# Six tiles of the second output block ahead of the gated mixer, and kept tiles for the down projection's last rows

## The chip, the cores and the metric

The kernel runs on one core of one Trainium2 chip. The time is device microseconds of one execution, taken as the median of several; the profile is one more execution, recorded by the hardware profiler. The engines of a core work side by side and wait for each other by semaphores: TensorE (PE, matrix products; its weight loads are PEld), VectorE (DVE), ScalarE (ACT), GpSimd (POOL), and SyncE (SP), which here only issues transfers between the device's memory (DRAM) and the on-chip memory. Products are added up in a separate small memory, PSUM.

## The reference

One decoder layer on 256 tokens of width 2048, in float32. A norm, one wide input projection, and two mixers (a gated delta rule over 16 heads and a causal pooling mixer) that are gated and added; an output projection with a residual; a norm, a gated MLP of width 5632 with a causal convolution, a down projection with a residual; a last norm.

```python
def reference(x, norm_mix_w, w_in, ..., w_out, norm_ffn_w, w_up, conv_ffn_w, conv_ffn_b, w_down, norm_final_w):
    ...
        mixed = jax.nn.sigmoid(g_a) * y_a + jax.nn.sigmoid(g_b) * y_b
        x = x + jnp.einsum('bsd,de->bse', mixed, w_out[l])
        h = rmsnorm(x, norm_ffn_w[l])
        gate, up = jnp.split(jnp.einsum('bsd,df->bsf', h, w_up[l]), 2, axis=-1)
        gate = causal_dwconv(gate, conv_ffn_w[l]) + conv_ffn_b[l]
        x = x + jnp.einsum('bsf,fd->bsd', jax.nn.gelu(gate, approximate=False) * up, w_down[l])
    return rmsnorm(x, norm_final_w)
```

## The kernel before

All weights pass once through one stream of tiles. A tile is 256 rows by 512 columns of a weight (two blocks of 128 rows, 512 KB). The list `srcs` fixes the order of the stream. For each tile, SP issues a load into one of four `raw` buffers (L112); ACT casts it into one of three `whi` buffers (L121); DVE subtracts that from `raw` into one of three `wlo` buffers (L128). `hi` and `lo` together carry the float32 value through products that keep fewer bits. `weights()` hands out the next tile and prepares the stream two tiles further.

A product of float32 quality is three matmuls: high part times `hi`, low part times `hi`, high part times `lo`. `gemm_a` (L158 to L160) does this for a block of 512 output columns: for each tile two row blocks and two halves of 128 tokens, twelve matmuls. A block of columns needs eight tiles where the depth is 2048, and its sums lie in one of two PSUM tiles `psm`.

Instructions are written in program order, and a scheduler with a simulated timeline orders them within each engine when the kernel is built. Each engine then works its own list off in order.

The mixers run in four groups of four heads. Each group yields four of the sixteen row blocks that the output projection multiplies (`mhi`, `mlo`). For the last group, `gated()` (L840, L841: the products that end in `sz`) and `mixed()` (eight PE transposes of `sz`, L203; the cast L853; the subtraction L854) come late. So the output projection starts early with what is ready: six tiles of column block 0 and two of block 1 (L864), whose rows belong to groups 0 to 2. The last two tiles of a block, rows of the fourth group, can be used only after `mixed()`. Then `xt`, the input x for the residual, is loaded by four transfers on ACT's queue (L872), and each finished block is added to it (L882, DVE), squared for the norm (L885, ACT), transposed (L891, PE), cast (L895) and split (L896).

The MLP follows, and then the down projection. It has 22 row steps `kp` of four tiles each, one for each block c of 512 columns; the sums of four blocks and two token halves t fill all eight PSUM banks. `down_part` (L945 to L947) is six matmuls: one tile, one token half. For the last row step, the tile of block 0 is used as it comes; the other three are used first for all of half 0 and then for half 1. Behind each half: the sum with the residual (L962, DVE) and the square (L964, ACT) per block, the mean over four columns (L966, L967, DVE), the power −1/2 (L968, POOL), the products with the last norm's weights `nfin` and with the scale (L971 and L975, DVE; L978, ACT), and four stores issued by SP (L979).

Of the kernel before, what the change touches and what calls it, by code (L numbers as in the profile page):

```python
# [7 lines left out]
F32 = mybir.dt.float32  # L8
# [5 lines left out]
P = 128  # L14
# [19 lines left out]
def kernel(  # L34
# [32 lines left out]
    def nm(s):  # L67
        cnt[0] += 1
        return f"{s}_{cnt[0]}"
# [45 lines left out]
    def begin(n):  # L115
        while len(made) < min(len(srcs), n):
            load(len(made) + 1)
            raw = loads[len(made)]
            shape = list(raw.shape)
            hi = wpool.tile(shape, F32R, tag="whi", name=nm("whi"))  # L120
            nc.scalar.copy(hi, raw)  # L121
            if shape[1] == 8:
                lo = None
                nc.vector.tensor_tensor(hi[:, :, 32:64], raw[:, :, 0:32], hi[:, :, 0:32].bitcast(F32),
                                        op=ALU.subtract)
            else:
                lo = wpool.tile(shape, F32R, tag="wlo", name=nm("wlo"))
                nc.vector.tensor_tensor(lo, raw, hi.bitcast(F32), op=ALU.subtract)  # L128
            made.append((hi, lo))

# [744 lines left out]
    ssq4 = cpool.tile([P, 2, 4], F32, tag="ssq4", name="ssq4b")  # L875
    for c in range(4):
        if c < 2:
            ps = gemm_a(at(mhi), at(mlo), KD, range((6, 2)[c], 8), early[c])
        else:
            ps = gemm_a(at(mhi), at(mlo), KD)  # L880
        xs = xt[:, :, c * 512 : (c + 1) * 512]
        nc.vector.tensor_tensor(xs, xs, ps, op=ALU.add)  # L882
        for t in range(2):
            jk = cpool.tile([P, 512], F32, tag="sqj", name=nm("sqj"))
            nc.scalar.activation(jk, xs[:, t, :], AF.Square, accum_out=ssq4[:, t, c : c + 1])  # L885
        for k2 in range(2):
# [59 lines left out]
            mm(acc[c][t], ll(k, t), hi[:, kk, :], start=False, stop=False)  # L946
            mm(acc[c][t], lh(k, t), lo[:, kk, :], start=False, stop=(k == KF - 1))  # L947

    LAST = KF // 2 - 1
# [6 lines left out]
    ssq5 = cpool.tile([P, 2, 4], F32, name="ssq5")  # L956
    for t in range(2):
        for c in range(1, 4):
            down_part(LAST, c, t, *ws[c - 1])
        for c in range(4):  # L960
            xs = xt[:, t, c * 512 : (c + 1) * 512]
            nc.vector.scalar_tensor_tensor(xs, acc[c][t], rs2[:, t : t + 1], xs, op0=ALU.mult, op1=ALU.add)  # L962
            jk = cpool.tile([P, 512], F32, tag="sqj", name=nm("sqj"))
            nc.scalar.activation(jk, xs, AF.Square, accum_out=ssq5[:, t, c : c + 1])  # L964
        rs = cpool.tile([P, 1], F32, name=nm("rs"))
        nc.vector.tensor_reduce(rs, ssq5[:, t, :], axis=mybir.AxisListType.X, op=ALU.add)  # L966
        nc.vector.tensor_scalar(rs, rs, 1.0 / D, EPS, op0=ALU.mult, op1=ALU.add)  # L967
        nc.gpsimd.tensor_tensor(rs, rs, epsx[:, 0:1], op=ALU.pow)  # L968
        for c in (2, 3):
            xs = xt[:, t, c * 512 : (c + 1) * 512]  # L970
            nc.vector.tensor_tensor(xs, xs, nfin[:, c * 512 : (c + 1) * 512], op=ALU.mult)  # L971
        for c in (0, 2, 1, 3):
            xs = xt[:, t, c * 512 : (c + 1) * 512]
            if c < 2:
                nc.vector.scalar_tensor_tensor(xs, xs, rs, nfin[:, c * 512 : (c + 1) * 512],  # L975
                                               op0=ALU.mult, op1=ALU.mult)
            else:
                nc.scalar.activation(xs, xs, AF.Copy, scale=rs)  # L978
            nc.sync.dma_start(out[0, t * P : (t + 1) * P, c * 512 : (c + 1) * 512], xs)  # L979


# [29 lines left out]
```

## Time and profile before

| | us |
|---|---|
| median of 3 runs | 1581.47 (1581.29 to 1581.65) |
| the profiled execution | 1581.2 |
| its span, first to last instruction | 1579.4 |
| PE busy | 1565.1 |
| DVE busy | 1066.2 |
| ACT busy | 745.4 |
| output projection: first and last matmul | 733.6 to 835.5 |
| last load of the weight stream issued | 1551.8 |

The span is shorter than the execution by what lies ahead of the first and behind the last recorded instruction. Matmuls overlap in PE's pipeline, so a matmul of 0.39 us can start every 0.23 us; the pitch of the starts tells PE's pace, and the busy time tells only whether it stood still. The granted clock was 0.998 over the span. In a row of a timeline, the bracket at the end names how long the engine had been idle before and what released it.

### The profile page before, as it was taken

The numbers are of one execution on the slowest core, as the hardware profiler recorded it, in microseconds if no ns is written. First come the engines' busy times: TensorE is split into PE (matmuls) and PEld (weight loads), VectorE is DVE, ScalarE is ACT, GpSimd is POOL, SyncE is SP. The second block draws the span as 40 slices with busy tenths as digits, with TensorE's granted clock in tenths as the row PEclk, the third lists the DMA queues.
The fourth block names the chain that finished last, engine by engine and source line by source line (L and its number), as shares of the span: only waits on it lengthen the run. The fifth ranks groups of instructions, "written<-read, shape, count | busy, mean of one in ns | idle before, by whom it ended". The sixth has DMA issues, their size and how long they took to land.

```text
span 1579.4 us, 21330 instructions
## 1 busy us (share of the span) xinstructions
PE 1565.1 (99%) x8086; PEld 1315.5 (83%) x8086; DVE 1066.2 (68%) x1619; ACT 745.4 (47%) x954; POOL 45.0 (3%) x69
## 2 busy tenths in 40 slices
PE   9999999999999999999999999999999999999997
PEld 8878888888878888788788888888888888888885
DVE  6897758885798657785556667766666667444445
ACT  6454445544555445544454544444444444434344
POOL 3010000000000000000000000000000000000000
PEclk9999999999999999999999999999999999999999
DMA  8776657675667647775656666666666666666663
GB/s 261 207 233 187 185 160 209 206 213 170 180 210 205 199 137 208 218 199 169 197 181 183 188 188 188 191 191 189 186 188 188 188 190 214 195 196 191 196 189 132
DMA packets 167925, 304.22 MB, mean 193 GB/s; under 512 B 19187, under 2 KB 22275, under 8 KB 167695
## 3 DMA queue, kind: packets, MB, share of 16 engines
q1 hardware_dynamic: 165088, 298.36, 64.1%
q10 hardware_dynamic: 2734, 4.51, 0.9%
q8 instruction: 63, 1.03, 0.3%
q14 instruction: 40, 0.32, 0.1%
HBM read 297.56 MB, written 5.27 MB: 192 GB/s over the span
## 4 chain that ended last, share of the span: by engine, by line
PE 96%; DVE 1%; DMA 1%; issue 1%; ACT 0%; DVEq 0%; POOLq 0%; POOL 0%; SPq 0%
PE psm L160 14%; PE psm L159 14%; PE psm L158 14%; PE psm L182 10%; PE psg L182 10%; PE psg L183 5%; PE psm L183 5%; PE psg L945 3%; PE psg L946 3%; PE psg L947 3%; PE psm L945 2%; PE psm L947 2%; PE psm L946 2%; PE psm L285 1%; PE psg L620 1%
## 5 line engine op out<-in xcount | busy, mean ns | idle before, releaser
L128 DVE TENSOR_TENSOR wlo<-raw,whi 128x1024 fp32r<-128x1024 f32 x528 | 645.1, 1223 | 421.0 <-ACT whi L121 412.1
L121 ACT CAST whi<-raw 128x1024 fp32r<-128x1024 f32 x530 | 557.6, 1053 | 737.9 <-PE psm L159 308.4
L160 PE MATMUL psm<-wlo,xhl 128*128 128x512 f32 x864 | 339.5, 393 | 0.7 <-DVE wlo L128 0.7
L158 PE MATMUL psm<-whi,xhl 128*128 128x512 f32 x864 | 339.0, 392 | 0.0
L159 PE MATMUL psm<-whi,xhl 128*128 128x512 f32 x864 | 338.4, 392 | 0.0
L182 PE MATMUL psm<-fhl,whi 128*128 128x512 f32 x704 | 246.2, 396 | 0.0
L182 PE MATMUL psg<-fhl,whi 128*128 128x512 f32 x704 | 238.0, 394 | 0.0
L183 PE MATMUL psm<-fhl,wlo 128*128 128x256 f32 x704 | 194.4, 279 | 0.0
L160 PEld LDWEIGHTS psm<-wlo,xhl 128*128 128x128 f32 x864 | 162.3, 188 | 34.3 <-DVE wlo L128 1.4
L159 PEld LDWEIGHTS psm<-whi,xhl 128*128 128x128 f32 x864 | 162.2, 188 | 33.4
L158 PEld LDWEIGHTS psm<-whi,xhl 128*128 128x128 f32 x864 | 162.3, 188 | 32.9 <-issue 0.2
L183 PE MATMUL psg<-fhl,wlo 128*128 128x256 f32 x704 | 178.7, 279 | 0.0
L182 PEld LDWEIGHTS psm<-fhl,whi 128*128 128x128 f32 x704 | 131.4, 188 | 30.5
L182 PEld LDWEIGHTS psg<-fhl,whi 128*128 128x128 f32 x704 | 129.2, 188 | 24.2
L183 PEld LDWEIGHTS psg<-fhl,wlo 128*128 128x128 f32 x704 | 132.5, 188 | 6.9
L183 PEld LDWEIGHTS psm<-fhl,wlo 128*128 128x128 f32 x704 | 132.5, 188 | 1.1
L945 PE MATMUL psg<-whi,hhi 128*128 128x512 f32 x176 | 68.6, 390 | 0.0
L945 PE MATMUL psm<-whi,hhi 128*128 128x512 f32 x176 | 68.5, 389 | 0.0
L946 PE MATMUL psm<-whi,hlo 128*128 128x512 f32 x176 | 68.5, 389 | 0.0
L946 PE MATMUL psg<-whi,hlo 128*128 128x512 f32 x176 | 68.5, 389 | 0.0
L947 PE MATMUL psm<-wlo,hhi 128*128 128x512 f32 x176 | 68.5, 389 | 0.0
L947 PE MATMUL psg<-wlo,hhi 128*128 128x512 f32 x176 | 61.7, 389 | 0.0
(241 smaller groups left out, 1489.7 us busy)
## 6 DMA issues: line engine op xcount, KB each, us to landing
raw<-in_w_in_dram SPq DMA_DIRECT2D x226, 512.0 KB, 4.3
raw<-in_w_up_dram SPq DMA_DIRECT2D x176, 512.0 KB, 4.5
raw<-in_w_down_dram SPq DMA_DIRECT2D x88, 512.0 KB, 4.4
raw<-in_w_out_dram SPq DMA_DIRECT2D x32, 512.0 KB, 3.9
mv<-vrow SPq DMA_DIRECT2D x12, 512.0 KB, 5.1
taps<-in_conv_qkv_w_dram SPq DMA_DIRECT2D x16, 256.0 KB, 6.0
raw<-in_pool_w_dram SPq DMA_DIRECT2D x8, 512.0 KB, 6.0
x<-in_x_dram SPq DMA_DIRECT2D x4, 512.0 KB, 8.2
```

The costliest lines, as they stand in the source:

```text
L121: nc.scalar.copy(hi, raw)
L128: nc.vector.tensor_tensor(lo, raw, hi.bitcast(F32), op=ALU.subtract)
L158: mm(ps[:, t, :], lh(k, t), hi[:, kk, :], start=(k == 0), stop=False)
L159: mm(ps[:, t, :], ll(k, t), hi[:, kk, :], start=False, stop=False)
L160: mm(ps[:, t, :], lh(k, t), lo[:, kk, :], start=False, stop=(k == nk - 1))
L182: mm(ps[f], hi[:, kk, fs], rhl(k), start=(k == 0), stop=False, skip_group_check=True)
L183: mm(ps[f][:, 1, :], lo[:, kk, fs], rhl(k)[:, 0, :], start=False, stop=(k == nk - 1), skip_group_check=True)
L285: mm(ps_k0[:, t, :], part(k, t), w[:, kk, :], start=(k == 0 and w is hi and part is xh), stop=(k == KD - 1 and w is lo))
L620: mm(pg0, kq[:, h, 0, 0:P], kq[:, h, :, :], start=True, stop=True)
L945: mm(acc[c][t], lh(k, t), hi[:, kk, :], start=(k == 0), stop=False)
L946: mm(acc[c][t], ll(k, t), hi[:, kk, :], start=False, stop=False)
L947: mm(acc[c][t], lh(k, t), lo[:, kk, :], start=False, stop=(k == KF - 1))
```

## The change

Three edits.

In the output projection, six tiles of block 1 come ahead of `gated()` and `mixed()` in program order instead of two, and the list of the stream is changed to match: six tiles of block 0, six of block 1, the last two of block 0, the last two of block 1.

In the down projection, the four tiles of the last row step (`LAST`, 21) are taken from the end of the stream and put in behind the row steps 9, 12, 15 and 18, one each. Their `hi` and `lo` go to buffers of their own, `khi` and `klo`, in the places that held row blocks of the MLP's result which the down projection has by then used (`mtile` 0 to 7).

At the end, the last two row steps are done block by block for each token half: for block c the tile of row step 20 and then the kept tile of row step 21. The tile of block 0 in row step 20 is used for both halves at once. Sum, square and product with `nfin` follow each block as it is done; for block 3 the product with `nfin` is merged with the scale. The mean is made from a partial sum over three blocks (`part`) and the fourth square. Blocks 2 and 3 are scaled on DVE, blocks 0 and 1 on ACT; three stores go to SP's queue and the fourth to ACT's.

```diff
-    srcs += outw[0][:6] + outw[1][:2] + outw[0][6:] + outw[1][2:] + outw[2] + outw[3]
+    srcs += outw[0][:6] + outw[1][:6] + outw[0][6:] + outw[1][6:] + outw[2] + outw[3]
...
-    srcs += [down[c][kp] for kp in range(KF // 2) for c in range(4)]
+    LAST = KF // 2 - 1
+    KEEP = (9, 12, 15, 18)
+    kept = {}
+    for kp in range(LAST):
+        srcs += [down[c][kp] for c in range(4)]
+        if kp in KEEP:
+            kept[len(srcs)] = KEEP.index(kp)
+            srcs.append(down[KEEP.index(kp)][LAST])
...
-            hi = wpool.tile(shape, F32R, tag="whi", name=nm("whi"))
+            keep = kept.get(len(made))
+            hi = wpool.tile(shape, F32R, tag="whi", name=nm("whi")) if keep is None else \
+                mtile(keep, shape, F32R, nm("khi"))
...
-    early = [gemm_a(at(mhi), at(mlo), KD, range(n)) for n in (6, 2)]
+    early = [gemm_a(at(mhi), at(mlo), KD, range(n)) for n in (6, 6)]
...
-            ps = gemm_a(at(mhi), at(mlo), KD, range((6, 2)[c], 8), early[c])
+            ps = gemm_a(at(mhi), at(mlo), KD, range(6, 8), early[c])
...
-    for kp in range(LAST + 1):
-        for c in range(4 if kp < LAST else 1):
+    wk = []
+    for kp in range(LAST - 1):
+        for c in range(4):
             w = weights()
             for t in range(2):
                 down_part(kp, c, t, *w)
-    ws = [weights() for c in range(3)]
+        if kp in KEEP:
+            wk.append(weights())
+    ws = []
+    for c in range(4):
+        ws.append(weights())
+        if c == 0:
+            for t in range(2):
+                down_part(LAST - 1, c, t, *ws[c])
...
     for t in range(2):
-        for c in range(1, 4):
-            down_part(LAST, c, t, *ws[c - 1])
         for c in range(4):
+            if c:
+                down_part(LAST - 1, c, t, *ws[c])
+            down_part(LAST, c, t, *wk[c])
...
+            if c < 3:
+                nc.vector.tensor_tensor(xs, xs, nfin[:, c * 512 : (c + 1) * 512], op=ALU.mult)
+            if c == 2:
+                nc.vector.tensor_reduce(part[:, ts], ssq5[:, t, 0:3], axis=mybir.AxisListType.X, op=ALU.add)
+                nc.vector.tensor_scalar(part[:, ts], part[:, ts], 1.0 / D, EPS, op0=ALU.mult, op1=ALU.add)
+        nc.vector.tensor_scalar(rs[:, ts], ssq5[:, t, 3:4], 1.0 / D, part[:, ts], op0=ALU.mult, op1=ALU.add)
+        nc.gpsimd.tensor_tensor(rs[:, ts], rs[:, ts], epsx[:, 0:1], op=ALU.pow)
+        scaled(2, nc.vector, nc.sync)
+        scaled(0, nc.scalar, nc.sync)
+        scaled(3, nc.vector, nc.sync)
+        scaled(1, nc.scalar, nc.scalar)
```

`scaled(c, by, queue)` multiplies block c in place by the scale (on ACT; on DVE with `tensor_scalar` for block 2; on DVE together with `nfin` for block 3) and issues its store on the given queue.

More of the change, by code (lines that the diff above doesn't have):

```diff
@@ L126, in begin @@
             else:
-                lo = wpool.tile(shape, F32R, tag="wlo", name=nm("wlo"))
+                lo = wpool.tile(shape, F32R, tag="wlo", name=nm("wlo")) if keep is None else \
+                    mtile(4 + keep, shape, F32R, nm("klo"))
                 nc.vector.tensor_tensor(lo, raw, hi.bitcast(F32), op=ALU.subtract)
@@ L954, with scaled @@
                 down_part(kp, c, t, *w)
-    ws = [weights() for c in range(3)]
+        if kp in KEEP:
[6 more added lines that the diff above has]
+                down_part(LAST - 1, c, t, *ws[c])
     ssq5 = cpool.tile([P, 2, 4], F32, name="ssq5")
+    part = cpool.tile([P, 2], F32, name="part")
+    rs = cpool.tile([P, 2], F32, name="rsf")
     for t in range(2):
-        for c in range(1, 4):
-            down_part(LAST, c, t, *ws[c - 1])
+        ts = slice(t, t + 1)
+        def scaled(c, by, queue):
+            xs = xt[:, t, c * 512 : (c + 1) * 512]
+            if by is nc.scalar:
+                nc.scalar.activation(xs, xs, AF.Copy, scale=rs[:, ts])
+            elif c < 3:
+                nc.vector.tensor_scalar(xs, xs, rs[:, ts], None, op0=ALU.mult)
+            else:
+                nc.vector.scalar_tensor_tensor(xs, xs, rs[:, ts], nfin[:, c * 512 : (c + 1) * 512],
+                                               op0=ALU.mult, op1=ALU.mult)
+            queue.dma_start(out[0, t * P : (t + 1) * P, c * 512 : (c + 1) * 512], xs)
@@ L966 @@
[L966 to L979, printed above, removed]
+            if c < 3:
+                nc.vector.tensor_tensor(xs, xs, nfin[:, c * 512 : (c + 1) * 512], op=ALU.mult)
```

4 lines of the change are left out of this document (1 added, 3 removed).

## The prediction

> **What bounds the kernel now.** I read the page first, then the waits of the matmul engine, then two stretches of the timeline, where the waits lie and where the program ends.
>
> ```profile
> span 1579.4 us, 21330 instructions
> PE 1565.1 (99%) x8086; PEld 1315.5 (83%) x8086; DVE 1066.2 (68%) x1619; ACT 745.4 (47%) x954; POOL 45.0 (3%) x69
> ```
>
> PE is busy for 99% of the span, so only two things can shorten the kernel: PE's waits, and the time when PE has stopped or not yet begun. The change adds and removes no matmul, only reorders them. PE's waits by cause (us in total, times, longest):
>
> ```profile
> PE psm L160 <- DVE wlo L128: 1.5, 3, 0.7
> PE psm L158 <- ACT whi L121: 0.9, 1, 0.9
> ```
>
> Of these 2.4 us, 0.91 + 0.52 + 0.28 = 1.71 lie in one place, in the output projection (columns: start, duration, engine, line):
>
> ```profile
> 763.63 0.39 PE L160 MATMUL psm<-wlo,mhi 128*128 128x512 f32 x1
> 763.83 1.04 ACT L121 CAST whi<-raw 128x1024 fp32r<-128x1024 f32 x1 [1.67 <-PE psm L159]
> 764.90 1.22 DVE L128 TENSOR_TENSOR wlo<-raw,whi 128x1024 fp32r<-128x1024 f32 x1 [0.29 <-ACT whi L121]
> 764.93 0.50 PE L158 MATMUL psm<-whi,mhi 128*128 128x512 f32 x1 [0.91 <-ACT whi L121]
> 765.26 0.40 PE L159 MATMUL psm<-whi,mlo 128*128 128x512 f32 x1
> 766.18 0.50 PE L160 MATMUL psm<-wlo,mhi 128*128 128x512 f32 x1 [0.52 <-DVE wlo L128]
> 766.52 0.40 PE L158 MATMUL psm<-whi,mhi 128*128 128x512 f32 x1
> 767.30 1.23 DVE L841 TENSOR_TENSOR sz<-sz,yb 128x1024 f32<-128x1024 f32 x1
> 768.36 0.39 PE L160 MATMUL psm<-wlo,mhi 128*128 128x512 f32 x1
> 768.56 1.05 ACT L121 CAST whi<-raw 128x1024 fp32r<-128x1024 f32 x1 [3.68 <-DVE sz L841]
> 768.67 1.06 PE L203 MATMUL psg<-ident,sz 128*128 128x128 f32 x8
> 769.84 0.39 ACTq L872 DMA_DIRECT2D xt<-in_x_dram  x1
> 770.23 0.41 PE L158 MATMUL psm<-whi,mhi 128*128 128x512 f32 x1
> 770.78 1.28 DVE L854 TENSOR_TENSOR mlo<-psg,mhi 128x512 fp32r<-128x512 f32 x2
> 770.92 0.50 PE L160 MATMUL psm<-wlo,mhi 128*128 128x512 f32 x1 [0.28 <-DVE wlo L128]
> 771.26 0.40 PE L158 MATMUL psm<-whi,mhi 128*128 128x512 f32 x1
> ```
>
> The stream has only three `whi` buffers. Behind the two early tiles of block 1 it brings the last two tiles of block 0, which nobody can use before `mixed()` has made the fourth group. They hold two buffers; the third alone goes round. So the cast at 763.83 begins when PE leaves the tile before, and PE waits for the whole cast and then for the subtraction of L128.
>
> The end of the program:
>
> ```profile
> 1566.02 0.75 DVE L962 SCALAR_TENSOR_TENSOR xt<-psm,rs,xt 128x512 f32<-128x512 f32 x1 [0.61 <-PE psm L947]
> 1566.86 0.63 ACT L964 ACTIVATE sqj<-xt 128x512 f32<-128x512 f32 x1 [0.64 <-DVE xt L962]
> 1568.31 0.39 PE L947 MATMUL psm<-wlo,hhi 128*128 128x512 f32 x1
> 1568.77 0.74 DVE L962 SCALAR_TENSOR_TENSOR xt<-psm,rs,xt 128x512 f32<-128x512 f32 x1
> 1569.51 1.41 DVE L975 SCALAR_TENSOR_TENSOR xt<-xt,rs,nfin 128x512 f32<-128x512 f32 x2
> 1569.76 1.32 ACT L978 ACTIVATE xt<-xt,rs 128x512 f32<-128x512 f32 x2
> 1570.98 0.61 ACT L964 ACTIVATE sqj<-xt 128x512 f32<-128x512 f32 x1
> 1571.50 0.19 ACT L964 ACTIVATION_READ_ACCUMULATOR sqj<-xt 128x1 f32 x1
> 1572.39 0.15 DVE L967 TENSOR_SCALAR rs<-rs 128x1 f32<-128x1 f32 x1
> 1572.62 0.55 POOL L968 TENSOR_TENSOR rs<-rs,epsx 128x1 f32<-128x1 f32 x1 [3.14 <-DVE rs L967]
> 1573.21 1.33 ACT L978 ACTIVATE xt<-xt,rs 128x512 f32<-128x512 f32 x2 [1.52 <-POOL rs L968]
> 1573.21 1.41 DVE L975 SCALAR_TENSOR_TENSOR xt<-xt,rs,nfin 128x512 f32<-128x512 f32 x2 [0.67 <-POOL rs L968]
> 1573.95 1.80 SPq L979 DMA_DIRECT2D out_dram<-xt  x4
> ```
>
> The last product ends at 1568.31 + 0.39 = 1568.70. The last square could follow its sum at 1569.51, but ACT is scaling the first row half (L978) and starts it at 1570.98. The scale of the second half is in use at 1573.21, 4.51 us after the last product.
>
> **The change, part by part.**
>
> *Output projection.* In the built order PE now runs five whole tiles of block 1 and the first two matmuls of a sixth ahead of the transposes of L203; then the rest of the sixth, the two tiles of block 0, the last two of block 1. The stream has the same order, so no buffer is held by a tile that must wait, and casts run two tiles ahead. A matmul's pitch is (768.36 − 766.52) / 8 = 0.23 us. What exceeds it in the rows above: 763.63 to 764.93, 1.07; to 765.26, 0.10; to 766.18, 0.69; to 766.52, 0.11; 770.23 to 770.92, 0.46; to 771.26, 0.11. Together 2.54 us, which I take whole. The turn into the transposes and out of them stays.
>
> What could be late next. `sz` is ready at 767.30 + 1.23 = 768.53; PE comes for it after 39 pitches from 763.63, at 772.6: 4 us of margin. The narrowest cover is the split of the fourth group: on DVE the last L128 before L854 needs a cast that waits for PE to leave the fourth of the five tiles. By pitch of twelve matmuls (2.72) that cast starts near 772.1, L128 ends near 774.5, and L854's first half (0.64) near 775.1. PE needs it after the transposes (1.3 with the turns) and ten matmuls (2.3), near 776.2. Margin about 1.1 us; what exceeds it PE waits in full. Behind L854 stand L128s of later tiles, two tiles from use.
>
> The `xt` loads (L872, on ACT's queue behind L853) move with the transposes, about 4 us later:
>
> ```profile
> xt<-in_x_dram ACTq DMA_DIRECT2D x4, 512.0 KB, 9.8
> ```
>
> Issued near 773.8, landed by 783.6 at that rate. The first sum (L882) could start at 781.6, when the two tiles of block 0 are through; at worst it is 2 us late, with the L128s of the next block's tiles behind it on DVE. PE needs the first of those after two more tiles, near 787.1; it would end at 783.6 + 1.22 + 1.22 = 786.0. Cost nothing, cover 1.1 us.
>
> *Kept tiles.* Four of the 88 tiles of the down projection are loaded, cast and split after rows 9, 12, 15, 18 instead of last, so four times the stream does a tile for which PE has no work.
>
> ```profile
> 1554.91 1.05 ACT L121 CAST whi<-raw 128x1024 fp32r<-128x1024 f32 x1 [1.67 <-PE psm L946]
> 1556.00 1.22 DVE L128 TENSOR_TENSOR wlo<-raw,whi 128x1024 fp32r<-128x1024 f32 x1 [1.50 <-ACT whi L121]
> raw<-in_w_down_dram SPq DMA_DIRECT2D x88, 512.0 KB, 4.4
> ```
>
> Per tile (2.72) ACT idles 1.67 and DVE 1.50; the extra cast (1.05) and subtraction (1.22) fit into one such pause, in their own buffers. On SP's queue the extra load takes one of four `raw` buffers, so the next loads start one turn later. A load has four turns (10.9) less cast and subtraction (2.3) and landing (4.4): 4.2 us spare, then 1.5. Behind that PE has casts two tiles ahead. Twelve tiles lie between kept ones, so the spare comes back. Cost 0; if the stream had no spare, a turn for each, 4 × 2.72 = 10.9 us.
>
> *The end.* PE does the same matmuls, now column by column for each half, so the first half's scaling falls beside the second half's 42 matmuls (9.7 us), and the sum over three columns is there before the last product ends. Left behind that: start of the sum 0.07 (1568.70 to 1568.77), sum 0.75, to the square 0.09 (1566.77 to 1566.86), square with its read 0.71 (1570.98 to 1571.69), to DVE 0.05 (my estimate, from gaps of 0.04 to 0.09 here), one small operation 0.15, to POOL 0.08, power 0.55, to its users 0.04: 2.49 instead of 4.51, a gain of 2.02 us. Bounds: 1.3 if each hand-over costs 0.2, 2.2 if the unshown one is nothing.
>
> *The stores.* SP had four issues in 1.80 us; now three, and ACT issues the fourth. That looks like half a microsecond, but
>
> ```profile
> 1574.80:1577.50 2.70, 0.00 (x0) 0.00 (x0) 0.00 (x0) 0.00 (x0) 0.00 (x0) 0.50 0.99 376
> ```
>
> the DMA engines are full (0.99, 376 GB/s) while the four stores run: 4 × 128 × 512 × 4 bytes at that rate take 2.8 us, more than their issuing. So the first store's start counts, 0.74 us behind the scale's first use before. The Trainium skill ("Trainium Kernel Development and Optimization", Key Constraints) says that DMAs issued from SP, ACT and POOL run on the same 16 engines and that several issuers save only issue time; by it the second queue brings nothing here, against 0.5 us by counting issues, and the full engines of the row above agree with it.
>
> The first store now waits for a `tensor_scalar` of 128x512 on DVE, which no row has:
>
> ```profile
> L914 DVE TENSOR_SCALAR y<-gs,cfw,vec 128x256 f32<-128x256 f32 x44 | 15.1, 407 | 0.0
> L192 DVE TENSOR_TENSOR gs<-psm,lh 128x256 f32<-128x256 f32 x44 | 17.4, 416 | 0.0
> ```
>
> At half the width it costs 0.41, as much as an operation on two tensors, so I take about 0.68; bounds 0.41 and 0.75. With 0.68 the first store starts 0.70 behind the scale: gain 0.04. Bounds: a loss of 0.3, if the store on ACT's queue lands last, and a gain of 0.35. The Trainium skill ("VectorE: DVE Perf Modes", Mode 2×_2P) says that an fp32 `tensor_scalar` in SBUF runs at twice the rate of an operation on two tensors; by it the first store would start 0.3 us earlier. The two rows above, equal to 2%, do not show it.
>
> *Sum.* 2.54 + 2.02 + 0.04 = 4.6 us. The profiled execution took 1581.2 us, its span 1579.4; 1.8 lies outside and stays. The median of the runs is 1581.47, 0.27 above, so the forecast is 1576.6 for such an execution and 1576.9 for a median.
>
> **The rivals.**
>
> A, the wait moves: the fourth group's split or `xt` comes later than the covers of 1.1 us, and what PE saved ahead of the transposes it waits behind them. For it: DVE serves L128, L854 and L882 in one order, and the margins are the smallest anywhere. Against: each was reckoned with the later value. Only the end's gain is left: 1581.47 − 2.06 = 1579.4.
>
> B, the end does not shorten: DVE or ACT holds the last column's sum or square behind work that the new order puts there (the products with `nfin`, the second half's scaling). For it: that is what happened before. Against: the built order has only small sums ahead of the last sum. 1581.47 − 2.54 = 1578.9.
>
> C, slower: around the kept tiles the stream is the bound, not PE. Place: the load after a kept tile. Price: a turn each, 10.9 us, less 4.6: 1587.8. It decides where a load takes more than 4.4 + 1.5 us to land and the casts' lead of two tiles is used up too; for it speaks that beside the `xt` loads 9.8 us were needed, against it that nothing else loads in that stage and that ACT waits for PE there, not for a DMA.
>
> D, the change does nothing: the scheduler might undo the order. The built order shows both moves; 1581.5.
>
> E, the store rule: the fp32 `tensor_scalar` takes 0.34 instead of 0.68, and the first store and the end come 0.3 us earlier: 1576.6.
>
> **How the numbers follow.** Forecast 0.71, E 0.06, A 0.09, B 0.05, C 0.08, D 0.01. A measurement of this kernel tells about 0.2% from no change, 3.2 us: below 1578.3 is faster. Forecast and E make 0.77 faster; A, B, D 0.15 the same; C 0.08 slower. The range: the unknown costs reach from 4.6 down to 3.6 (hand-overs 0.7, ACT's store 0.3) and up to 5.2 (0.35, 0.2), and 0.3 is for the spread of runs, which gives 1576.0 to 1578.2; up to 1579.0 it takes in B, and 1575.6 leaves room for a turn at the transposes that goes too (0.2). A, C and D, 0.18, stay out.
>
> **What would show it.** Right: PE's waits on L121 and L128 gone between 758 and 790 us; matmuls without pause from row 9 to the end; 2.4 to 2.6 us from the last product to the first use of the scale; DMA engines full for 2.8 us at the end. Wrong: PE waiting for `mlo`, `xt` or `whi` behind the transposes (A); ACT's last square starting over 0.2 us after its sum (B); ACT waiting for `raw` in the down projection (C). A span over 1576.5 would mean that one of the two terms did not come (the forecast's is 1574.8).

## The result, and the profile after

The changed kernel takes 1576.38 us (median of 7 runs, 1575.81 to 1577.52), the kernel before 1581.47 (7 runs beside them, 1581.1 to 1582.61): a ratio of 0.9968, 95% interval 0.9958 to 0.9977, or 5.1 us less. The forecast was 1576.9 with a range of 1575.6 to 1579.0. In a second series the ratio was 0.9965 (0.9951 to 0.9979), 5.3 us less.

The profiled execution of the changed kernel took 1577.52 us, the slowest of its seven. The head of its page, and the largest of PE's waits by cause (us in total, times, longest):

```profile
span 1575.6 us, 21329 instructions
PE 1563.7 (99%) x8086; PEld 1315.0 (83%) x8086; DVE 1067.5 (68%) x1623; ACT 745.3 (47%) x954; POOL 45.0 (3%) x69
```

```profile
PE psm L171 <- DVE wlo L139: 1.5, 3, 0.7
```

The wait for a cast in the output projection (0.9, L158 before) is gone. Of the three waits for `wlo` of before, two lay in the output projection and one at 658 us, in the mixers, which the change doesn't touch. The two are gone and the one is still there; two others, at 310 and 649 us, also in the mixers, have come. These two put this execution back by 0.81 and 0.27 us against the one before; with smaller differences elsewhere in the mixers its output projection begins at 735.05, against 733.56, 1.49 us behind. In the second series' profile of the same kernel the wait at 310 did not come, so it is not what the change does. In the ten other kernels below that have the same code up to there it began between 733.4 and 735.0. So two spans can't be compared as they stand; the parts can. (L131, L139 and L169 to L171 are now the cast, the subtraction and `gemm_a`; L956 to L958 `down_part`; L214 the transposes; L864, L865 and L883 what were L853, L854 and L872.)

The windows of the output projection around the transposes, first of the kernel before, then of the changed one (us, then busy time of PE, PEld, DVE, ACT, POOL):

```profile
758.00:790.00 32.00, 30.29 (x140) 23.98 (x140) 19.49 (x25) 13.85 (x20) 1.64 (x1) 1.00 0.65 212
```

```profile
758.00:790.00 32.00, 32.00 (x158) 26.95 (x158) 20.95 (x24) 13.95 (x19) 1.63 (x1) 1.00 0.64 215
```

PE stood still for 1.71 of 32 us before, for nothing after. The timeline of the changed kernel at the same place:

```profile
773.48 1.05 ACT L131 CAST whi<-raw 128x1024 fp32r<-128x1024 f32 x1 [1.67 <-PE psm L170]
773.74 0.39 PE L170 MATMUL psm<-whi,mlo 128*128 128x512 f32 x1
773.97 1.03 PE L214 MATMUL psg<-ident,sz 128*128 128x128 f32 x8
774.56 1.23 DVE L139 TENSOR_TENSOR wlo<-raw,whi 128x1024 fp32r<-128x1024 f32 x1 [1.49 <-PE psg L214]
774.76 0.48 PE L171 MATMUL psm<-wlo,mhi 128*128 128x512 f32 x1
775.07 0.39 PE L169 MATMUL psm<-whi,mhi 128*128 128x512 f32 x1
775.71 0.68 DVE L865 TENSOR_TENSOR mlo<-psg,mhi 128x512 fp32r<-128x512 f32 x1
```

The cast again waits 1.67 us for PE and not PE for the cast; PE leaves the stream for the transposes and comes back with no bracket. First to last matmul of the output projection now takes 98.95 us instead of 101.90.

The end of the changed kernel:

```profile
1566.84 0.39 PE L958 MATMUL psm<-klo,hhi 128*128 128x512 f32 x1
1567.26 0.75 DVE L998 SCALAR_TENSOR_TENSOR xt<-psm,rs,xt 128x512 f32<-128x512 f32 x1 [0.17 <-PE psm L958]
1568.11 0.63 ACT L1000 ACTIVATE sqj<-xt 128x512 f32<-128x512 f32 x1 [2.00 <-DVE xt L998]
1568.64 0.19 ACT L1000 ACTIVATION_READ_ACCUMULATOR sqj<-xt 128x1 f32 x1
1568.86 0.21 DVE L1006 TENSOR_SCALAR rsf<-ssq,part 128x1 f32<-128x1 f32 x1 [0.85 <-ACT sqj L1000]
1569.15 0.55 POOL L1007 TENSOR_TENSOR rsf<-rsf,epsx 128x1 f32<-128x1 f32 x1 [8.55 <-DVE rsf L1006]
1569.74 1.34 ACT L985 ACTIVATE xt<-xt,rsf 128x512 f32<-128x512 f32 x2 [0.91 <-POOL rsf L1007]
1569.74 0.49 DVE L987 TENSOR_SCALAR xt<-xt,rsf 128x512 f32<-128x512 f32 x1 [0.67 <-POOL rsf L1007]
1570.26 1.30 SPq L991 DMA_DIRECT2D out_dram<-xt  x3
1571.11 0.37 ACTq L991 DMA_DIRECT2D out_dram<-xt  x1
```

From the last product's end (1566.84 + 0.39 = 1567.23) to the first use of the scale are 2.51 us instead of 4.51. The square follows its sum at once. ACT had been idle for 2.00 us before it; in the kernel before it was scaling the other half then. The first store comes 0.52 us behind the first use, and from one microsecond behind its issue on the DMA engines are full (share 1.02, 379 GB/s):

```profile
1571.26:1573.76 2.50, 0.00 (x0) 0.00 (x0) 0.00 (x0) 0.00 (x0) 0.00 (x0) 0.50 1.02 379
```

One view shows something that the prediction had called a sign against it: ACT does wait for loads in the down projection. Around one of the kept tiles, ACT's timeline; and the sum over all four, from the answer for `khi`:

```profile
1455.52 1.05 ACT L131 CAST whi<-raw 128x1024 fp32r<-128x1024 f32 x1 [1.67 <-PE psm L957]
1459.34 1.05 ACT L131 CAST khi<-raw 128x1024 fp32r<-128x1024 f32 x1 [2.77 <-DMA raw<-in_w_down_dram]
1460.30 1.99 ACT L131 CAST whi<-raw 128x1024 fp32r<-128x1024 f32 x2
```

```profile
  DMA raw<-in_w_down_dram: 10.2, 4
```

The scheduler has put each kept cast ahead of the casts of the two tiles in front of it, because a kept cast needs no free `whi` buffer. ACT works its list in order, so it stands at the kept cast until that load has landed, and the two casts that it passed follow back to back. PE has no wait there: its lead of two tiles covers it. In the second series' profile the four kept casts waited 3.10 to 3.23 us each, and PE again did not. The experiments ask how far that holds.

### The profile page after: what moved, and what is told of

Same layout as the page of the kernel before. It is cut to its first block, busy times and chain, and to the rows that moved or that the text cites. A ratio compares the mean times of both kernels' runs of the same rounds, so it can differ in the third digit from the quotient of the medians.

```text
span 1575.6 us, 21329 instructions
## 1 busy us (share of the span) xinstructions
PE 1563.7 (99%) x8086; PEld 1315.0 (83%) x8086; DVE 1067.5 (68%) x1623; ACT 745.3 (47%) x954; POOL 45.0 (3%) x69
## 4 chain that ended last, share of the span: by engine, by line
PE 97%; issue 1%; DMA 1%; DVE 1%; ACT 0%; POOLq 0%; POOL 0%; SPq 0%; DVEq 0%
PE psm L171 14%; PE psm L170 14%; PE psm L169 14%; PE psm L193 10%; PE psg L193 10%; PE psg L194 5%; PE psm L194 5%; PE psg L956 2%; PE psg L958 2%; PE psg L957 2%; PE psm L958 2%; PE psm L957 2%; PE psm L956 2%; PE psm L296 1%; PE psg L631 1%
## 5 line engine op out<-in xcount | busy, mean ns | idle before, releaser
L139 DVE TENSOR_TENSOR wlo<-raw,whi 128x1024 fp32r<-128x1024 f32 x524 | 640.1, 1223 | 399.9 <-ACT whi L131 388.4
L131 ACT CAST whi<-raw 128x1024 fp32r<-128x1024 f32 x526 | 553.3, 1053 | 717.4 <-PE psm L170 314.0
L171 PE MATMUL psm<-wlo,xhl 128*128 128x512 f32 x864 | 339.6, 393 | 1.5 <-DVE wlo L139 1.5
L169 PE MATMUL psm<-whi,xhl 128*128 128x512 f32 x864 | 339.0, 392 | 0.0
L171 PEld LDWEIGHTS psm<-wlo,xhl 128*128 128x128 f32 x864 | 162.3, 188 | 35.6 <-DVE wlo L139 2.9
L169 PEld LDWEIGHTS psm<-whi,xhl 128*128 128x128 f32 x864 | 162.3, 188 | 32.9 <-issue 0.2
L956 PE MATMUL psg<-whi,hhi 128*128 128x512 f32 x168 | 65.5, 390 | 0.0
L956 PE MATMUL psm<-whi,hhi 128*128 128x512 f32 x168 | 65.4, 389 | 0.0
L958 PE MATMUL psm<-wlo,hhi 128*128 128x512 f32 x168 | 65.4, 389 | 0.0
L958 PE MATMUL psg<-wlo,hhi 128*128 128x512 f32 x168 | 59.0, 389 | 0.0
```

The lines of the kernel that those rows point to most:

```text
L169: mm(ps[:, t, :], lh(k, t), hi[:, kk, :], start=(k == 0), stop=False)
L171: mm(ps[:, t, :], lh(k, t), lo[:, kk, :], start=False, stop=(k == nk - 1))
L956: mm(acc[c][t], lh(k, t), hi[:, kk, :], start=(k == 0), stop=False)
```

## The experiments

Each kernel ran beside the kernel before, on the same chip; kernels that are compared closely ran in one series where that is said. Differences are shown against the changed kernel, and times against the kernel before of the same series.

### The output projection alone, and the down projection with the end alone

The first keeps only the new order of the output projection, the second only the rest.

```diff
# output projection alone: the down projection and the end as before
-    for kp in range(LAST):
-        srcs += [down[c][kp] for c in range(4)]
-        if kp in KEEP:
...
+    srcs += [down[c][kp] for kp in range(KF // 2) for c in range(4)]
...
# down projection and end alone: the output projection as before
-    srcs += outw[0][:6] + outw[1][:6] + outw[0][6:] + outw[1][6:] + outw[2] + outw[3]
+    srcs += outw[0][:6] + outw[1][:2] + outw[0][6:] + outw[1][2:] + outw[2] + outw[3]
-    early = [gemm_a(at(mhi), at(mlo), KD, range(n)) for n in (6, 6)]
+    early = [gemm_a(at(mhi), at(mlo), KD, range(n)) for n in (6, 2)]
```

> The kernel before with the output projection's edit alone (six tiles of block 1 ahead, stream order to match); down projection and end as before. Theory: all of the wait around the transposes goes and nothing gives it back, 2.5 to 3.0 us, so about 1578.6; the profile has no PE pause between the last group's gating and the end of the output projection, and 4.5 us from the last product to the first use of the last scale, as before. Rival (A): the wait moves behind the transposes or is given back in the MLP, under 1 us gained, 1580.5 or more.

> The kernel before with the down projection's edits alone (kept tiles, block by block at the end, new scaling and stores); output projection as before. Theory: 2.3 us gained, all behind the last product, so about 1579.2, with the three PE pauses in the output projection as before; 2.5 us from the last product to the first use of the scale, and no PE pause between row steps 9 and 21. Rival (C): the stream is short of time behind the kept tiles, PE pauses there and the gain is under 1 us or a loss, 1580.5 or more.

Measured: 1579.09 us (1578.48 to 1580.37), ratio 0.9983 (0.9974 to 0.9992), for the output projection alone; 1579.49 (1578.02 to 1580.81), the same ratio and interval, for the rest alone; 1581.86 for the kernel before. That is 2.8 and 2.4 us less, together 5.1, as much as the whole change. The output projection takes 98.95 us in the first and 101.87 in the second, as in the kernels after and before. The two edits are independent as far as the times tell (each ratio is uncertain by 1.4 us), and the parts of the profiles say the same: neither gives anything back.

### The end in its new order, without kept tiles

```diff
-        if kp in KEEP:
-            kept[len(srcs)] = KEEP.index(kp)
-            srcs.append(down[KEEP.index(kp)][LAST])
...
+    for kp in range(LAST + 1):
+        for c in range(4 if kp < LAST else 1):
...
-                down_part(LAST - 1, c, t, *ws[c])
-            down_part(LAST, c, t, *wk[c])
+                down_part(LAST, c, t, *ws[c])
```

The last row step stands at the end of the stream again. Sum, square and product still follow block by block, with the partial mean and the stores of the changed kernel. The text below says that the output projection is as before; the kernel that ran had the new one, so its 2.8 us have to be taken off first, and the expected times stand for a kernel that much slower.

> As the run with the down projection's edits alone, but without kept tiles: stream and matmuls of the last row steps in the order of before (the last row's tile of block 0 as it comes, the other three for each half), only the sums, scaling and stores are the new ones. Here the first half ends 18 matmuls (4.1 us) before the second. Output projection as before. Theory: the first half's scaling falls into the second half's last sums, but the partial sum takes most of the chain off the end: 2.5 to 3.4 us from the last product to the first use of the scale, 1.3 to 2.1 us gained, about 1579.8. Rival: the block order, which needs the kept tiles, makes the gain; without it ACT is busy with the first half as before, 4.0 to 4.5 us, gain under 0.6 us, 1580.9 or more.

Measured: 1578.49 us (1577.89 to 1580.16), ratio 0.998 (0.9971 to 0.9989), 3.4 us less than before, of which the output projection makes 2.8; about 0.6 are left for the end. In the profiles it is 0.32: from the last matmul's start to the end of the span it takes 10.77 us, against 11.09 before and 8.76 in the changed kernel. The rows show why the rest did not come:

```profile
1565.59 0.39 PE L953 MATMUL psm<-wlo,hhi 128*128 128x512 f32 x1
1566.39 0.74 DVE L982 SCALAR_TENSOR_TENSOR xt<-psm,rs,xt 128x512 f32<-128x512 f32 x1
1567.13 1.33 ACT L970 ACTIVATE xt<-xt,rsf 128x512 f32<-128x512 f32 x2
1568.37 0.61 ACT L984 ACTIVATE sqj<-xt 128x512 f32<-128x512 f32 x1
1569.62 0.21 DVE L990 TENSOR_SCALAR rsf<-ssq,part 128x1 f32<-128x1 f32 x1
1570.50 1.33 ACT L970 ACTIVATE xt<-xt,rsf 128x512 f32<-128x512 f32 x2 [1.42 <-POOL rsf L991]
```

From the last product (1565.59 + 0.39 = 1565.98) to the first use are 4.52 us, as before the change: ACT scales the first half (1567.13) ahead of the last square (1568.37). Without kept tiles the second half has 18 matmuls, 4.1 us, and the first half's scale comes too late to be used beside them. The 0.32 us lie behind the first use, in the stores, which are the changed kernel's. My theory, that the new order of sums, squares and scales makes the gain, is wrong; the kept tiles make it, by giving the second half 42 matmuls. Whether an order forced on ACT, the last square ahead of the first half's scaling, would shorten the end without kept tiles was not run.

### Four tiles ahead instead of six

```diff
-    srcs += outw[0][:6] + outw[1][:6] + outw[0][6:] + outw[1][6:] + outw[2] + outw[3]
+    srcs += outw[0][:6] + outw[1][:4] + outw[0][6:] + outw[1][4:] + outw[2] + outw[3]
```

> The changed kernel with four instead of six tiles of block 1 ahead of the gating, stream order to match. Theory: PE reaches the transposes 5.4 us earlier than with six, near 767, before the products that end in sz are done (768.5), and then meets the tiles whose split is not ready, so it waits 1.0 to 2.5 us there: 1577.4 to 1579.0. Rival: six are more than needed, and four leave no wait: within 0.4 us of the changed kernel, about 1576.4.

Measured: 1577.91 us (1577.28 to 1578.24), ratio 0.9974 (0.9964 to 0.9985); 3.9 us less than before, 1.2 less gain than six tiles bring. The output projection takes 99.87 us, 0.92 more than with six, a little below the theory's lower end:

```profile
770.78 0.41 PE L169 MATMUL psm<-whi,mhi 128*128 128x512 f32 x1
771.33 1.28 DVE L865 TENSOR_TENSOR mlo<-psg,mhi 128x512 fp32r<-128x512 f32 x2
771.47 0.50 PE L171 MATMUL psm<-wlo,mhi 128*128 128x512 f32 x1 [0.28 <-DVE wlo L139]
```

With four ahead the transposes begin at 769.14, only 0.76 us after `sz` is ready (768.38), where six leave 3.94. So PE does not come ahead of `sz`, as I had expected, and the waits of 0.91 and 0.52 us ahead of the transposes are gone with four tiles too. What is left is one wait for a `wlo` behind the transposes, 0.57 us with the slow matmul after it, and a turn at the transposes of 1.63 us instead of 1.33. Four tiles are too few; five were not tried. Another 0.3 us went in the down projection, where a kept tile's load took longer than in the changed kernel's first profile (5.75 us from its issue to the cast, 4.21 there):

```profile
1460.13 1.05 ACT L131 CAST khi<-raw 128x1024 fp32r<-128x1024 f32 x1 [4.31 <-DMA raw<-in_w_down_dram]
1463.18 0.39 PE L957 MATMUL psm<-whi,hlo 128*128 128x512 f32 x1
1463.63 0.50 PE L958 MATMUL psm<-wlo,hhi 128*128 128x512 f32 x1
```

ACT stood for 4.31 us ahead of a kept cast, and PE came to a `wlo` that was not there: a pitch of 0.45 instead of 0.23, and a slow next one. Where the longest wait was 3.23 us (the second run of the changed kernel) nothing was lost; at 4.31 it was.

### Every kept cast in its turn

```diff
-            nc.scalar.copy(hi, raw)
+            if keep is None:
+                last_cast[0] = nc.scalar.copy(hi, raw).ins
+            else:
+                with tc.issue_after(last_cast[0]):
+                    nc.scalar.copy(hi, raw)
```

> The changed kernel with the cast of each kept tile held to its turn: it may be issued only behind the cast of the tile ahead of it in the stream. In the changed kernel the scheduler puts it ahead of the casts of the two tiles before it, and ACT waits there 2 to 3 us for its load. Theory: in its turn the kept tile's load has landed long before, so ACT's idle time ahead of the kept cast falls from 2.2 to 2.9 us to under 1.8 us with no wait for a load, and the spare time that the prediction reckoned is there; the time stays within 0.4 us, since PE did not wait in the changed kernel either. Rival: the kept load is late by itself, and ACT waits for it in any place.

Measured: 1576.67 us (1575.91 to 1576.79), ratio 0.9966 (0.9953 to 0.9978). The changed kernel, in the same series, took 1576.39. On ACT:

```profile
1426.97 1.05 ACT L133 CAST whi<-raw 128x1024 fp32r<-128x1024 f32 x1 [1.67 <-PE psg L962]
1427.92 1.05 ACT L136 CAST khi<-raw 128x1024 fp32r<-128x1024 f32 x1
```

The kept cast now runs directly behind the cast ahead of it, without any wait: its load had landed. The landings in this run's trace give the spare, from the landing of a tile to its cast: 4.1 us for tiles of the down projection away from the kept ones (the median; 4.2 reckoned), 2.0 to 2.5 for the four kept tiles, at the least 0.5 to 1.0, for the third tile behind a kept one (1.5 reckoned), and over 3 again from the fifth. So the spare is there much as the prediction had it, and it comes back; the changed kernel spends it by the order of ACT's list, not by the loads. The time doesn't move, as expected.

### Four kept tiles in a row

```diff
-        if kp in KEEP:
-            kept[len(srcs)] = KEEP.index(kp)
-            srcs.append(down[KEEP.index(kp)][LAST])
+        for c in range(4 if kp == 18 else 0):
+            kept[len(srcs)] = c
+            srcs.append(down[c][LAST])
```

This tests the distance between kept tiles, once with the scheduler's order of casts and once with every cast in its turn.

> The changed kernel, but all four kept tiles stand in the stream in a row behind row step 18 instead of one each behind 9, 12, 15 and 18. The work is the same; only the distance goes. The built order on ACT again puts casts of kept tiles ahead of the casts of the tiles in front of them (khi, whi, khi, whi, khi, khi, whi), because a kept cast needs no free whi buffer. Theory: each such cast waits for its load, about 3 us as at the single kept tiles, and the casts that PE needs next wait behind it on the same engine; with four in a row PE's lead of casts is used up. PE waits for whi or wlo there, 3 to 7 us in all, and the kernel takes 1579.5 to 1583.5 us. Rival (the prediction's step): the stream has 4.2 us to spare in its loads and PE two tiles of lead, four tiles in a row cost 6.9 us of stream, so PE waits at most 1 us: 1576.0 to 1577.5 us.

> As the kernel with the four kept tiles in a row behind row step 18, but every cast of the stream is held to the order of the stream on ACT, so that no kept cast goes ahead of an earlier tile's. Theory (the queue's order on ACT, not the loads, is what a kept tile spends): the loads come one in about 1.7 us where buffers are free, four extra tiles cost 4 x 1.7 = 6.9 us of stream, against 4.2 us of spare and 3.6 us or more of lead of the casts: PE waits 0 to 1 us and the kernel takes 1576.0 to 1577.5 us. Rival (an extra tile costs a whole turn of 2.72 us, the stream having no spare): 10.9 us less the lead, PE waits 3 us or more: from 1579.5 us up.

Measured: 1579.27 us (1578.0 to 1581.98), ratio 0.9985 (0.9976 to 0.9994), in the scheduler's order; 1578.97 (1577.45 to 1582.02), 0.9987 (0.9978 to 0.9996), in turn. By the ratios that is 2.7 and 3.0 us more than the changed kernel (each of the ratios, the changed kernel's too, is uncertain by 1.4 us). In the profiles PE loses 2.4 and 1.9 us at one place (the pitches of 2.21, 0.34, 0.45, 0.34 and of 1.69, 0.34, 0.46, 0.34 us, each less 0.23), and nothing elsewhere behind the mixers. Here PE waits for a cast, by the waits of the kernel in turn:

```profile
PE psg L961 <- ACT whi L133: 1.3, 1, 1.3
```

```profile
1525.23 1.05 ACT L133 CAST whi<-raw 128x1024 fp32r<-128x1024 f32 x1 [1.67 <-PE psg L962]
1526.18 2.00 ACT L136 CAST khi<-raw 128x1024 fp32r<-128x1024 f32 x2
1529.65 1.05 ACT L136 CAST khi<-raw 128x1024 fp32r<-128x1024 f32 x1 [1.46 <-DMA raw<-in_w_down_dram]
1532.34 1.05 ACT L136 CAST khi<-raw 128x1024 fp32r<-128x1024 f32 x1 [1.64 <-DMA raw<-in_w_down_dram]
1533.78 1.04 ACT L133 CAST whi<-raw 128x1024 fp32r<-128x1024 f32 x1 [0.40 <-DMA raw<-in_w_down_dram]
```

Both theories missed, and both rivals: PE lost less than the 3 us of the first theory and the second rival, and more than the 1 us of the others. The two runs say why. The first two kept tiles are cast at once, one behind the other; the third and the fourth wait for their loads. A load is issued when a subtraction frees a `raw` buffer, and the buffers ahead of the row came free at the old pitch of 2.72 us: the fourth kept tile's load was issued at 1527.57, landed 4.74 us later at 1532.31, and was cast at 1532.34. So four tiles put the next cast off from 1527.95 (1525.23 + 2.72) to 1533.78, by 5.8 us, not by 6.9 − 4.2 = 2.7. The spare of 4.2 us belongs to a load, and a row of tiles has it only once. Nor do the loads of the row come at the 1.7 us each that both texts reckoned with: the third and the fourth kept cast, each begun as its load landed, lie 2.69 us apart. Against that PE had a lead of 4.4 us (it needed the cast at 1533.42; at the usual pitch it would have ended at 1529.0). The difference, 1.4, and the wait for `wlo` behind it are the 1.9 us. The order of ACT's list, which I had made the main cause, costs the 0.5 us between the two runs in the profiles; in the times it is not seen.

### The last store on SP's queue

```diff
-        scaled(1, nc.scalar, nc.scalar)
+        scaled(1, nc.scalar, nc.sync)
```

> The changed kernel with the fourth store of each half back on SP's queue. Theory: the DMA engines are full while the stores run, so the queue does not count: 4.6 to 4.9 us from the first use of the last scale to the last landing, as with ACT's queue (4.7), time within 0.3 us of the changed kernel. Rival: issuing counts, the fourth store begins half a microsecond later and so does the end: 5.1 us or more.

Measured: 1576.85 us (1576.28 to 1577.09), ratio 0.9967 (0.9955 to 0.998), beside 0.9965 for the changed kernel. From the power's end to the last landing 4.86 us, against 4.76 in the changed kernel of the same series. From the first store's issue to the last landing it is 4.31, as in the kernel before, against 4.21. The four issues take 1.80 us on SP again, but the engines are as full as with two queues (share 0.98, 368 GB/s):

```profile
1569.73:1572.53 2.80, 0.00 (x0) 0.00 (x0) 0.00 (x0) 0.07 (x1) 0.00 (x0) 0.58 0.98 368
```

The second queue is worth 0.1 us, and no difference that the time shows. The rule weighed in the prediction (the Trainium skill, "Trainium Kernel Development and Optimization", Key Constraints: several issuers save only issue time) holds here: of the half microsecond of issuing that is saved, 0.1 us reaches the end.

### A longer pause before the mixers' decay rows are read

This tries for the waits at 310, 649 and 658 us that the profile after had shown: a step of the mixers yields seven times instead of five before it reads rows that come by DMA.

```diff
-WAIT = 5
+WAIT = 7
...
-        for _ in range(WAIT - 3):
+        for _ in range(2):
```

> The changed kernel with two more side steps between the round trip of a group's blocks through DRAM and the DVE work that reads them back (the constant that counts them 7 instead of 5; the second such wait as before). In the profile of the changed kernel PE waited once 0.8 us and once 0.3 us for L139 behind such a read. Theory: these waits are chance and go when DVE comes later to the read; sz of the last group is then ready up to 2.7 us later, which six tiles ahead (4 us of margin) still cover: 0.3 to 1.5 us faster than the changed kernel. Rival: the later end of the last group reaches PE, or the waits have another cause: no gain, or up to 1.5 us slower.

Measured: 1576.83 us (1576.27 to 1576.98), ratio 0.9967 (0.9954 to 0.9979). PE still waits there:

```profile
PE psm L171 <- DVE wlo L139: 0.7, 1, 0.7
```

The wait at 658 us is there with its full pitch of 1.05, and one of 0.45 at 310. The theory fails. The wait of 0.65 us at 310 in the first profile of the changed kernel is not in its second one either, so its shrinking here tells nothing. What brings the wait at 658, which every kernel here shows, the one before too, stays open.

### The end in halves

The last block of the second half is summed and squared in two halves, and block 2 is scaled and stored in two halves; the kept casts are in turn.

```diff
+            if c == 3 and t == 1:
+                for h in range(2):
+                    xh2 = xt[:, t, c * 512 + 256 * h : c * 512 + 256 * h + 256]
+                    nc.vector.scalar_tensor_tensor(xh2, acc[c][t][:, 256 * h : 256 * h + 256], rs2[:, ts], xh2, ...)
+                    ...
+                    nc.scalar.activation(jk, xh2, AF.Square, accum_out=ssqh[h])
...
+            if c == 2 and t == 1:
+                for h in range(2):
+                    o = c * 512 + 256 * h
+                    xh2 = xt[:, t, o : o + 256]
+                    nc.vector.tensor_scalar(xh2, xh2, rs[:, ts], None, op0=ALU.mult)
+                    queue.dma_start(out[0, t * P : (t + 1) * P, o : o + 256], xh2)
```

> The changed kernel with every kept cast in its turn on ACT, and the end cut finer: the second half's last block is summed and squared in two halves of 256 columns, so that the square of the first half runs beside the sum of the second; and block 2 of the second half is scaled and stored in two halves, so that the first store waits for 256 columns only. Theory (the chain of the end is a chain of single operations, and the DMA engines are full behind its first store): last product to first use of the scale 2.2 to 2.35 us instead of 2.5, first store 0.3 to 0.4 us behind that instead of 0.5; end 0.2 to 0.5 us earlier, 1576.0 to 1576.4 us where the changed kernel takes 1576.4. Rival (fixed costs eat it: two squares with two reads and one more small operation on DVE take as long as one square): end within 0.1 us of the changed kernel's, or later.

Measured: 1575.66 us (1575.12 to 1576.51), ratio 0.9963 (0.995 to 0.9975). The interval holds the changed kernel's 0.9968, so that it is faster than that one is not shown. The profile is shorter than that of the same kernel without halves by 0.44 us (spans of 1573.82 and 1574.26), but not at the end: between the output projection's last matmul and the down projection's first it takes 493.08 us, where every other kernel here takes 493.56. This edit doesn't touch that stage, and the cause stays open.

```profile
1565.00 0.39 PE L963 MATMUL psm<-klo,hhi 128*128 128x512 f32 x1
1567.77 1.33 ACT L998 ACTIVATE xt<-xt,rsf 128x512 f32<-128x512 f32 x2 [0.92 <-POOL rsf L1030]
1568.15 0.81 SPq L995 DMA_DIRECT2D out_dram<-xt  x2
```

From the last product (1565.39) to the scale 2.38 us, a little more than the 2.35 that I expected at most; the first store 0.38 behind it, as expected. But from the last matmul's start to the end of the span it is 8.82 us, against 8.77 in the same kernel without halves (1565.49 to 1574.26). What was won ahead of the stores the stores take back. Their first microsecond at work, with halves and without:

```profile
1569.15:1570.15 1.00, 0.00 (x0) 0.00 (x0) 0.00 (x0) 0.00 (x0) 0.00 (x0) 0.50 0.83 279
```

```profile
1569.91:1570.91 1.00, 0.00 (x0) 0.00 (x0) 0.00 (x0) 0.00 (x0) 0.00 (x0) 0.50 1.03 383
```

With halves the engines are not full at first (0.83) and move 279 GB/s. Shorter windows of the same stretch show two reasons:

```profile
1569.35:1569.55 0.20, 0.00 (x0) 0.00 (x0) 0.00 (x0) 0.00 (x0) 0.00 (x0) 0.50 0.51 169
1569.55:1569.75 0.20, 0.00 (x0) 0.00 (x0) 0.00 (x0) 0.00 (x0) 0.00 (x0) 0.50 1.03 348
```

The engines have too little to do between one small store and the next, which is issued 0.43 us behind it (0.51), and where they are full they move 348 GB/s in rows of half the length, against 373 to 389 without halves. The rival's result came, by another cause than it named. What each of the two reasons costs was not measured by a run of its own.

## Why the prediction was right, point by point

| term | predicted | measured |
|---|---|---|
| output projection | 2.54 | 2.95 (101.90 to 98.95) |
| last product to first use of the scale | 2.02 (4.51 to 2.49) | 2.00 (4.51 to 2.51) |
| stores | 0.04 | 0.34 (0.22 to the first issue, 0.12 to the last landing) |
| kept tiles | 0 | 0 |
| sum | 4.6 | 5.3 in the profiles, 5.1 and 5.3 in the medians |

*Output projection.* The pauses went, at the price put on them. The 0.41 beyond that is mostly the turn at the transposes, which I left in: from the last matmul ahead of them to the second behind them it took 1.64 us (768.36 to 770.00) and takes 1.33 (773.74 to 775.07). The range had 0.2 for this. The narrowest cover, reckoned at 1.1 us, was 0.97: the first half of L865 ended at 776.39 and PE used it at 777.36. The covers behind the transposes held: no bracket on PE names `mlo` or `xt`, and rival A had no part in it. The run with the output projection alone gives this term by itself, 2.8.

*The end.* The chain came within 0.02 us of its sum, though one item was off: the small operation took 0.21, not 0.15. It reads the partial sum, one value per partition, where the operation that I took the price from has constants alone; the last section has what such a value costs. The upper bound of 2.2 does not come out of the sum: with nothing for the hand-over that no row showed (0.05) the gain is 2.07. Rival B is out: the last square starts 0.10 us behind its sum. The reason that the prediction gave, 42 matmuls in the second half, is what the run without kept tiles confirms.

*The stores.* This is the term that was mis-sized. The `tensor_scalar` of 128x512 took 0.49 us where I took 0.68 from a row of half the width. The rule that I weighed against that row (the Trainium skill, "VectorE: DVE Perf Modes", Mode 2×_2P) gave 0.34, as I estimated it by halving the whole duration. The measurement lies between, 0.49 beside 0.69 for an operation on two tensors of the same shape (the product with `nfin`). But the rule is one of rate, and as such it holds here. The kernel with the end in halves has the same operation at half the width:

```profile
L994 DVE TENSOR_SCALAR xt<-xt,rsf 128x256 f32<-128x256 f32 x2 | 0.6, 350 | 0.7 <-POOL rsf L1030 0.7
```

From 256 to 512 columns it grows by 0.13 us (0.35 to 0.48), the operation on two tensors by 0.27 or 0.28 (0.42 to 0.69). The rest of the 0.48, about 0.22 us, does not depend on the width, and that is what halving left out. My row of half the width had two scalars per partition, and the prediction's "do not show it" was drawn from an operation that differs in more than its width. Rival E was right in its sign and mechanism and went too far by the fixed part. The other 0.12 us, a shorter time from the first issue to the last landing (1573.95 to 1578.26 before, 1570.26 to 1574.45 after), I had not foreseen; 0.1 us of it is what the store on ACT's queue is worth.

*Kept tiles.* The cost of 0 was right, and one step to it was not. I let the extra cast run in a pause of ACT with its load long there; in the kernel as built it goes ahead of two others and waits for the load, 10.2 us in four places. What hides that is PE's lead of two tiles, which I had only put "behind that". The sign that I named for rival C (ACT waiting for `raw`) therefore appeared without rival C: the sign would have had to be PE's wait, not ACT's. With the tiles in a row PE's wait does come, at 1.9 to 2.4 us, not at a turn for each (10.9): the price of C was too high, since the lead and the first load's spare are used up before PE pays.

*The profiled execution.* I forecast a span of 1574.8; it was 1575.6, since 1.49 us were lost ahead of the output projection and 0.7 more gained behind its start. The second run of the changed kernel, which began its output projection at 734.19, has a span of 1574.75.

## What to carry to other kernels

A tile that must wait should not sit in the small ring of buffers that everything else goes round in: put the consumer's order and the stream's order together so that a tile is brought only when it can be used. A tail shortens when the last part has enough matmuls to hide the part before it; reordering the small operations without that left the chain as long as it was (4.52 us beside 4.51). Extra tiles in a full stream cost nothing here at a distance of twelve tiles, and 1.9 to 2.4 us as four in a row; distances between were not run. A scheduler may let the kept tile go first on an in-order engine, so look at the built order and at the wait of the engine that is the bound, not at the waits of the others.

## What the runs showed of the hardware that was not expected

- `tensor_scalar` of 128x512 float32 on DVE with one scalar per partition took 0.48 to 0.49 us, `tensor_tensor` of the same shape 0.69 and `scalar_tensor_tensor` 0.75. At 128x256 the first took 0.35 and `tensor_tensor` 0.42: per column the first is twice as fast, and its fixed part is larger (about 0.22 us against 0.14).
- A scalar per partition came with about 0.06 us on DVE: `tensor_scalar` of 128x256 took 0.35 with one and 0.41 with two, and that of 128x1 0.15 with constants alone and 0.21 with one. No run varied the number of scalars and nothing else.
- After every wait of PE with a bracket in these profiles, from 20 us on, the next matmul's pitch is 0.34 us instead of 0.23, 0.11 us more. The bracket itself is short of the late start by 0.16, since it counts from the end of the matmul before and not from the pitch. At 771.47 with four tiles ahead the bracket says 0.28, and the two pitches around it, 0.69 and 0.34, exceed 0.23 by 0.57 together.
- Halving the first store made it start earlier and left the end where it was: for the first microsecond at work the DMA engines moved 279 GB/s instead of 383.
